# Mixture of experts in seven passes: the pass of the four smallest experts moves from fourth to sixth place

## The chip, the cores and the metric

The kernel runs on one core of a Trainium2 chip. The core has TensorE (matmuls), VectorE, ScalarE and GpSimd for elementwise work, SyncE, whose queue issues the large loads here, and 16 DMA engines. The metric is the device time of one execution in microseconds, as a median over runs.

## The reference

Two layers of a diffusion transformer over 256 latent tokens of 1024 features, with 256 context tokens beside them in the first layer. The first layer mixes tokens with latent attention and a gated linear recurrence, the second with a Hyena operator (long filters applied by Fourier transform between gates). Behind each mixer stands a mixture of 16 experts; each token takes two of them. Cut to what matters:

```
for layer in range(2):
    x = x + g1 * mixer[layer](modulate(rms_norm(x), sh1, sc1))
    h = modulate(rms_norm(x), sh2, sc2)
    gates = top2_in_best_group(sigmoid(h @ router_w))        # (256, 16)
    y = 0
    for e in range(16):
        act = silu(h @ w1[layer, e]) * (h @ w3[layer, e])    # 1024 -> 512
        y = y + gates[:, e:e+1] * (act @ w2[layer, e])       # 512 -> 1024
    x = x + g2 * y
return rms_norm(x, final_g)
```

Only the latent tokens' result is returned. All is float32. One expert has 6 MB of weights, one layer 96 MB, and no weight is used twice, so the two layers of experts fetch 192 MB from HBM.

## The kernel before

**Passes.** A layer of experts runs in seven passes, listed in `PASSES` (line 27). Six are pairs: two experts, with 64 token slots each, side by side in the 128 columns of TensorE. One is the quad: four experts with 32 slots each. Numbers 0 to 3 in the table are experts in a fixed order. Numbers 4 to 15 are places in an order sorted by token counts, which the kernel computes and loads into SyncE's registers (`chosen`); 4 to 7 are the four with fewest tokens. Both layers use the same table. In this text passes and places are counted from the first to the seventh; in the code `j` counts them from 0.

**One pass** (in `moe`) is: `up` with w1 (L1247, 64 matmuls for a quad, 32 for a pair), `silu`, `back` of the pass before (L1292, adds its result to x), fillers, `up` with w3, `times`, `turn` (transposes, L1262), fillers, `down` 0 and 1 with w2 (L1275) and `weigh`. In every second pass (`j` = 1, 3, 5) the tokens of the next two passes are fetched behind the w3 part: `place` builds a 0/1 matrix, `gather` multiplies it in (L1218), `slots` (L1234, L1236) makes the matrix and the gate values for the way back. So the gather for the fifth and sixth pass stands in the fourth place, and the gather for the seventh alone in the sixth.

**Fillers.** In the first layer `fill` runs pieces of the second layer's Hyena filters between these parts: an item is a filter step (L1439 two projections on TensorE, then eight VectorE instructions at L1448 to L1457 and one on GpSimd, then L1466 transposes and a copy on ScalarE) or a step of the Fourier butterflies (L1495, L1496). Its counts stand in `FJ`, one triple for each place, and belong to the place, whatever the pass. Places four and five have seven items each (in those with a gather one item is dropped from the second count), place six has five. In the second layer there are none.

**Weights.** `moe_tiles` lists a layer's weights as tiles of 1 MB, in the order of `PASSES`: for a pair 4 of w1, 4 of w3, 4 of w2; for the quad 8, 8 and 8; 98 loads for a layer, because four tiles of the last pass are cut in halves. In this text they are numbered from 0 in that order. `emit` (L219) issues them on SyncE, in order, from one queue; each waits there until the buffer that it goes to is free. In the first layer the buffers are a ring of ten in the steady state (nine of `w` and one of `x`), so that a tile can be issued when the tile ten places ahead has been used. In the second layer the ring has 18 (`sp`, `w` and `x`). An expert chosen by count has its address from a register; the tiles of the first two passes do not need it.

```
PASSES = ((0, 1), (2, 3), (8, 9), (4, 5, 6, 7), (10, 11), (12, 13), (14, 15))
FJ = ((0, 1, 1), (0, 1, 1), (1, 1, 2), (2, 3, 3), (1, 3, 3), (2, 1, 3), (2, 4, 1))
            fill(fills[j][0])
            up(j, "w3", first, firsts)
            times(j)
            if j % 2 and j < LAST:
                d = j // 2 + 1
                place(d, pos, firsts)
                gather(d, firsts)
```

The order of instructions on each engine is set by the order of the program and by a scheduler that moves single instructions a little; the order of weight tiles on SyncE follows `PASSES` alone.

Of the kernel before, what the change touches and what calls it, by code (L numbers as in the profile page):

```python
# [23 lines left out]
LOW = 32  # L24
STATIC = 4
DYN = 16 - STATIC
PASSES = ((0, 1), (2, 3), (8, 9), (4, 5, 6, 7), (10, 11), (12, 13), (14, 15))
LAST = len(PASSES) - 1
QUAD = 4
NW = 9  # L30
# [136 lines left out]
def build(tc, A, dbg=None, stop=None):  # L167
# [54 lines left out]
    def get(key):  # L222
        while key not in made:
            emit(1)
        used[0] = max(used[0], index[key] + 1)
        return made[key]
# [53 lines left out]
    def moe_tiles(l):  # L280
        for j, es_ in enumerate(PASSES):
            for nme in ("w1", "w3"):
                for kk in range(2):
                    for e in es_:
                        yield ((nme, l, e, kk), expert(nme, l, e, kk * 512, 4, 0, 512), (128, 4, 512))
            for h in range(2):
                for e in es_:
                    if j < LAST:
                        yield (("w2", l, e, h), expert("w2", l, e, h * 256, 2, 0, 1024), (128, 2, 1024))
                    elif h == 0:  # L290
                        yield (("w2", l, e, 0), expert("w2", l, e, 0, 4, 0, 512), (128, 4, 512))
            if j == LAST:
                for h in range(2):
                    for e in es_:
                        yield (("w2", l, e, 1 + h), expert("w2", l, e, h * 256, 2, 512, 512), (128, 2, 512))
# [875 lines left out]
    def moe(l, route, ws, filler=None, fills=((0, 0, 0),) * 8, budget=0, late=None, prepare=None, finish=None):  # L1171
# [22 lines left out]
        pairs = tuple(((2 * j, 2 * j + 1), CAP) for j in range(8))  # L1194
        firsts = tuple((es_, 128 // len(es_)) for es_ in PASSES)

# [114 lines left out]
        def first(nme, e, k, n=0):  # L1311
            if nme == "w2" and e in PASSES[LAST]:
                return get((nme, l, e, 1 + k // 2))[:, k % 2, :] if n else get((nme, l, e, 0))[:, k, :]
            nk = 2 if nme == "w2" else 4
            return get((nme, l, e, k // nk))[:, k % nk, n * 512:n * 512 + 512]
# [454 lines left out]
```

## Time and profile before

| | |
|---|---|
| time, median of 3 runs | 961.68 us (961.64, 965.34, 961.68) |
| the profiled execution's own time | 964.56 us |
| its span | 962.8 us |
| TensorE busy | 868.0 us, 90% |
| VectorE busy | 477.8 us, 50% |
| bytes moved | 289.33 MB, mean 301 GB/s |
| first layer of experts, on TensorE | 285.1 to 541.0 us |
| second layer of experts, on TensorE | 728.3 to 952 us |

The profile is of one execution; the span runs from its first to its last instruction. Busy time says how long an engine worked, not whether anyone waited for it; the waits and the stretches say that. The DMA share is the mean busy share of the 16 DMA engines, and rows that show a little more than 1 stand for full.

### The profile page before, as it was taken

The page shows a single profiled execution, that of the slowest core. Times are in us where ns is not written, and L with a number is a line of the kernel's source. Part 1 is how long each engine was busy: PE and PEld are TensorE (multiplying, and loading weights), DVE is VectorE, ACT ScalarE, POOL GpSimd, SP SyncE. Part 2 cuts the span into 40 slices and gives each one's busy share as a digit, 9 for nine tenths or more (in the row PEclk, how much of TensorE's full clock was granted, in tenths as well). Part 3 has the DMA queues.
Part 4 walks back from the last instruction along what each step waited for, and adds up shares of the span by engine and source line. Part 5 has one row for each costly group of instructions (what it writes and reads, how often), then busy time and mean ns, then how long its engine had stood idle before and what let it go on. Part 6 is the DMA issues. An engine that isn't in the chain of part 4 may idle for free. (4 is left out here: it accounts for less than half of the span.)

```text
span 962.8 us, 10887 instructions
## 1 busy us (share of the span) xinstructions
PE 868.0 (90%) x3992; PEld 458.1 (48%) x3992; DVE 477.8 (50%) x1119; ACT 231.9 (24%) x451; POOL 25.9 (3%) x29
## 2 busy tenths in 40 slices
PE   3898999999969999889999599999959999988984
PEld 1445755575543543433343288677545352422431
DVE  5349775763364445345622469976163241322123
ACT  3266414430231222122211312211031020100112
POOL 0000000000010000001100000000020000000000
PEclk9899999998969999999999799999978999999997
DMA  9946679469479889999999866842285999999994
GB/s 353 336 183 240 224 263 354 166 223 367 170 271 324 333 324 386 383 400 396 391 362 347 308 228 253 314 167 88 87 298 189 391 396 386 401 392 396 396 386 148
DMA packets 130568, 289.33 MB, mean 301 GB/s; under 512 B 6828, under 2 KB 8876, under 8 KB 130500
## 3 DMA queue, kind: packets, MB, share of 16 engines
q1 hardware_dynamic: 129428, 286.39, 81.5%
q10 hardware_dynamic: 1072, 2.10, 0.7%
q8 instruction: 35, 0.57, 0.2%
q14 instruction: 33, 0.27, 0.1%
HBM read 287.42 MB, written 1.05 MB: 300 GB/s over the span
## 5 line engine op out<-in xcount | busy, mean ns | idle before, releaser
L1247 PE MATMUL ps<-w,xe 128*64 128x512 f32 (+1 forms) x696 | 174.3, 597 | 2.8 <-DMA w<-in_moe_w 2.8
L1247 PEld LDWEIGHTS ps<-w,xe 128*64 128x64 f32 (+1 forms) x696 | 50.0, 129 | 88.0 <-issue 79.2
L1275 PE MATMUL ps<-w,at 128*64 128x512 f32 (+1 forms) x344 | 87.1, 597 | 4.5 <-DMA w<-in_moe_w 2.7
L1591 PE MATMUL ps<-xt,w 128*128 128x256 f32 x384 | 88.2, 388 | 1.8 <-ACT xt L1554 1.8
L1591 PEld LDWEIGHTS ps<-xt,w 128*128 128x128 f32 x384 | 74.2, 195 | 14.4 <-ACT xt L1554 2.1
L1294 DVE TENSOR_TENSOR x<-x,ps 128x512 f32<-128x512 f32 x56 | 37.0, 684 | 68.1 <-PE ps L1292 68.1
L442 DVE SCALAR_TENSOR_TENSOR e<-w,sg,e 128x512 f32<-128x512 f32 x91 | 67.0, 746 | 5.2 <-DMA w<-in_ada_w 4.1
L1281 DVE SCALAR_TENSOR_TENSOR ye<-ps,gs,grow 128x512 f32<-128x512 f32 x28 | 21.0, 748 | 83.9 <-PE ps L1275 83.9
L1247 PE MATMUL ps<-sp,xe 128*64 128x512 f32 (+1 forms) x216 | 55.5, 600 | 1.5 <-DMA sp<-in_moe_w 1.5
L1275 PEld LDWEIGHTS ps<-w,at 128*64 128x64 f32 (+1 forms) x344 | 26.9, 130 | 50.8 <-issue 40.3
L1283 ACT ACTIVATE yeh<-ye 128x512 fp32r<-128x512 f32 x28 | 17.6, 630 | 118.2 <-DVE ye L1281 118.2
L1257 DVE TENSOR_TENSOR th<-th,ps 128x512 f32<-128x512 f32 x14 | 9.6, 688 | 60.5 <-PE ps L1247 60.5
L1247 PE MATMUL ps<-x,xe 128*64 128x512 f32 (+1 forms) x112 | 37.5, 596 | 1.6 <-DMA x<-in_moe_w 1.6
L1218 PE MATMUL ps<-P,yh 128*128 128x256 f32 (+1 forms) x128 | 35.9, 313 | 2.8 <-DVE P L1203 2.8
L1218 PE MATMUL ps<-P,yl 128*128 128x256 f32 (+1 forms) x128 | 35.0, 307 | 0.0
L1223 ACT ACTIVATE xe<-ps,modc 128x256 f32<-128x256 f32 (+1 forms) x32 | 16.5, 540 | 70.0 <-DVE xe L1221 69.9
L1218 PEld LDWEIGHTS ps<-P,yh 128*128 128x128 f32 x128 | 27.9, 218 | 9.6 <-issue 7.1
L844 PE MATMUL ps<-hT,w 128*128 128x512 f32 x64 | 31.0, 643 | 1.2 <-DMA w<-in_ev_w_in 1.2
L1247 PEld LDWEIGHTS ps<-sp,xe 128*64 128x64 f32 (+1 forms) x216 | 16.0, 132 | 28.1 <-issue 24.4
L510 PE MATMUL ps<-w,x 128*128 128x512 f32 x64 | 28.4, 595 | 0.7 <-ACT x L1605 0.7
L510 PE MATMUL ps<-w,mix 128*128 128x512 f32 x64 | 28.8, 598 | 0.0
L1218 PEld LDWEIGHTS ps<-P,yl 128*128 128x128 f32 x128 | 27.8, 217 | 1.7 <-issue 1.7
(350 smaller groups left out, 1313.9 us busy)
## 6 DMA issues: line engine op xcount, KB each, us to landing
w<-in_moe_w SPq DMA_DIRECT2D x126, 1024.0 KB, 13.8
w<-in_ada_w SPq DMA_DIRECT2D x48, 1024.0 KB, 7.1
sp<-in_moe_w SPq DMA_DIRECT2D x41, 1024.0 KB, 14.2
x<-in_moe_w SPq DMA_DIRECT2D x21, 1024.0 KB, 14.5
w<-in_od_w_in SPq DMA_DIRECT2D x12, 1024.0 KB, 7.1
w<-in_ev_w_in SPq DMA_DIRECT2D x4, 1024.0 KB, 11.0
w<-in_ev_w_out SPq DMA_DIRECT2D x4, 1024.0 KB, 6.8
w<-in_moe_w SPq DMA_DIRECT2D x8, 512.0 KB, 9.8
```

The source lines that it names most:

```text
L442: V.scalar_tensor_tensor(eh, w[hf], c, eh, op0=OP.mult, op1=OP.add)
L510: T.matmul(po[t][n], a[:, k, t * 128:t * 128 + 128], b[:, n * 512:n * 512 + 512], start=(k == korder[0] and i == 0), stop=(k == korder[-1] ...
L844: T.matmul(uxp[b], get(("wux", hf))[:, k % 4, b * 128:b * 128 + 128], hT[hf][:, k % 4, :], start=(k == 0), stop=(k == KD - 1))
L1218: T.matmul(p[:, kk * w:kk * w + w], (yl if i % 2 else yh)[:, t, k * 128:k * 128 + 128], P[:, t, :w], start=(i == 0), stop=(i == 3))
L1223: S.activation(e[:, k, :w], p[:, w:2 * w], AF.Identity, scale=sc[:, k:k + 1], bias=sh[:, k:k + 1])
L1247: T.matmul(p[room * i:room * i + room, :], xe[j // 2][:, k, o:o + room], weight(nme, e, k), start=(k == 0), stop=(k == KD - 1), tile_posit ...
L1257: V.tensor_tensor(act[j], act[j], hid[j, "w3"], op=OP.mult)
L1275: T.matmul(p[room * i:room * i + room, :], act[j][:, o:o + room], weight("w2", e, k, n), start=(k == 0), stop=(k == 3), tile_position=(0, ...
L1281: V.scalar_tensor_tensor(e, po[j, n], gs[j], grow[l, 5][:, n * 512:n * 512 + 512], op0=OP.mult, op1=OP.mult)
L1283: S.activation(h, e, AF.Copy)
L1294: V.tensor_tensor(xs, xs, p, op=OP.add)
L1591: T.matmul(pb, w[:, k % 4, b * 128:b * 128 + 128], hT[:, k, :], start=(k == 0 and b % 2 == 0), stop=(k == KD - 1 and b % 2 == 1))
```

## The change

One line: the quad stands in the sixth place of the table, and the two pairs (10, 11) and (12, 13) move ahead of it. Each pass keeps its experts and its slots. What belongs to a place (the fillers, the gathers, the last pass's halves of w2) stays there.

```
-PASSES = ((0, 1), (2, 3), (8, 9), (4, 5, 6, 7), (10, 11), (12, 13), (14, 15))
+PASSES = ((0, 1), (2, 3), (8, 9), (10, 11), (12, 13), (4, 5, 6, 7), (14, 15))
```

TensorE, first layer, around the start of the fourth pass. Up to there its order is the same in both kernels. `w` is a weight tile, `xe` the gathered tokens, `at` the turned hidden values; 32x512 is a matmul for the 32 slots of one expert of the quad, 64x512 one for the 64 slots of an expert of a pair. Before:

```order
L1275 MATMUL ps_2369<-w_2355,at_2308 64x512
L1275 MATMUL ps_2369<-x_2358,at_2308 64x512
L1247 MATMUL ps_2384<-w_2385,xe_2047 32x512
L1247 MATMUL ps_2384<-w_2388,xe_2047 32x512
L1247 MATMUL ps_2384<-w_2391,xe_2047 32x512
L1292 MATMUL ps_2436<-yeh_2365,st_2093 128x512
L1292 MATMUL ps_2436<-yel_2367,st_2093 128x512
L1247 MATMUL ps_2384<-w_2394,xe_2047 32x512
```

With the change:

```order
L1275 MATMUL ps_2367<-w_2353,at_2306 64x512
L1275 MATMUL ps_2367<-x_2356,at_2306 64x512
L1247 MATMUL ps_2382<-w_2383,xe_2047 64x512
L1247 MATMUL ps_2382<-w_2386,xe_2047 64x512
L1247 MATMUL ps_2382<-w_2383,xe_2047 64x512
L1247 MATMUL ps_2382<-w_2386,xe_2047 64x512
L1247 MATMUL ps_2382<-w_2383,xe_2047 64x512
L1247 MATMUL ps_2382<-w_2386,xe_2047 64x512
```

Behind the same down matmuls stand a pair's matmuls, on two weight tiles in turn, where the quad's stood on four tiles in turn.

TensorE, first layer, behind the gather of the fourth pass: the slots (L1234, L1236), then fillers. `a2T` and `q` belong to the filter steps, `th` is the hidden part. Before:

```order
L1234 MATMUL ps_2585<-kc,P_2535 128x128 x2
L1236 MATMUL ps_2585<-rg_1524,P_2535 128x2 x2
L1234 MATMUL ps_2595<-kc,P_2535 128x128 x2
L1236 MATMUL ps_2595<-rg_1524,P_2535 128x2 x2
L1439 MATMUL ps_2605<-a2T,w_363_1927 128x256
L1247 MATMUL ps_2485<-w_2492,xe_2047 32x512
L1439 MATMUL ps_2606<-a2T,w_363_1927 128x256
L1466 MATMUL ps_2623<-kc,q_2474 128x128 x4
L1439 MATMUL ps_2629<-a2T,w_451_2311 128x256
L1247 MATMUL ps_2485<-w_2495,xe_2047 32x512
L1247 MATMUL ps_2485<-w_2486,xe_2047 32x512
L1247 MATMUL ps_2485<-w_2489,xe_2047 32x512
```

With the change:

```order
L1234 MATMUL ps_2545<-kc,P_2485 128x128 x2
L1236 MATMUL ps_2545<-rg_1524,P_2485 128x4 x2
L1439 MATMUL ps_2557<-a2T,w_363_1927 128x256
L1439 MATMUL ps_2558<-a2T,w_363_1927 128x256
L1466 MATMUL ps_2575<-kc,q_2448 128x128 x4
L1439 MATMUL ps_2581<-a2T,w_451_2309 128x256
L1439 MATMUL ps_2582<-a2T,w_451_2309 128x256
L1466 MATMUL ps_2599<-kc,q_2571 128x128 x4
L1262 MATMUL ps_2605<-kc,th_2407 128x128 x4
L1439 MATMUL ps_2616<-a2T,w_451_2309 128x256
L1439 MATMUL ps_2617<-a2T,w_451_2309 128x256
L1466 MATMUL ps_2634<-kc,q_2595 128x128 x4
```

Before, the fillers stood between the w3 matmuls of the quad. Now these are done ahead of the gather's end, and the filter steps stand one behind the other, with only the turn (L1262) between them.

SyncE, first layer, in the tiles of the fourth pass (128x4x512 is a tile of w1 or w3, 128x2x1024 one of w2; the rows of the ISA are waits). Before:

```order
L219 DMA w_2418<-in_moe_w 128x4x512
L219 ISA
L219 DMA w_2486<-in_moe_w 128x4x512
L219 ISA
L219 DMA w_2489<-in_moe_w 128x4x512
L219 ISA
L219 DMA w_2492<-in_moe_w 128x4x512
L219 ISA
L219 DMA w_2495<-in_moe_w 128x4x512
L219 ISA
L219 DMA w_2510<-in_moe_w 128x4x512
L219 ISA
```

With the change:

```order
L219 DMA w_2475<-in_moe_w 128x4x512
L219 ISA
L219 DMA w_2657<-in_moe_w 128x2x1024
L219 ISA
L219 DMA w_2660<-in_moe_w 128x2x1024
L219 ISA
L219 DMA w_2665<-in_moe_w 128x2x1024
L219 ISA
L219 DMA w_2668<-in_moe_w 128x2x1024
L219 ISA
L219 DMA w_2695<-in_moe_w 128x4x512
L219 ISA
```

At the same place in the queue the pair's four w2 tiles are reached after eight tiles of w1 and w3, where the quad had sixteen. The quad's 24 tiles come 24 tiles later. The number of tiles and of buffers is the same.

## Rows read from the trace of the kernel before

**Rows 1.** The page: busy tenths in 40 slices of the span.
```profile
PE   3898999999969999889999599999959999988984
...
DMA  9946679469479889999999866842285999999994
```

**Rows 2.** First layer's passes: length, PE, PEld, DVE, ACT, POOL busy (instructions), clock, DMA share, GB/s.
```profile
285.10:303.90 18.80, 18.62 (x92) 6.66 (x93) 7.25 (x23) 1.31 (x4) 0.97 (x1) 1.00 0.71 243
303.90:335.10 31.20, 31.20 (x164) 15.42 (x162) 13.76 (x34) 7.40 (x15) 0.74 (x1) 1.00 0.96 359
335.10:370.10 35.00, 34.15 (x156) 13.67 (x152) 16.97 (x39) 6.94 (x13) 2.42 (x3) 1.00 0.89 324
370.10:428.90 58.80, 53.50 (x295) 21.18 (x293) 23.80 (x59) 13.44 (x27) 3.48 (x4) 1.00 1.04 390
428.90:467.20 38.30, 37.19 (x157) 14.87 (x157) 23.51 (x55) 10.21 (x20) 4.47 (x5) 1.00 1.04 393
467.20:507.20 40.00, 37.96 (x173) 16.95 (x172) 15.06 (x32) 6.89 (x14) 1.69 (x2) 1.00 0.99 370
507.20:541.00 33.80, 31.32 (x134) 11.88 (x130) 12.74 (x22) 8.22 (x18) 0.00 (x0) 1.00 0.99 363
```

**Rows 3.** TensorE's waits, 370.1 to 428.9: who waited for whom, total, times, longest.
```profile
PE ps L1247 <- DMA w<-in_moe_w: 1.9, 1, 1.9
PE ps L1275 <- DMA w<-in_moe_w: 1.3, 2, 0.7
```

**Rows 4.** SyncE's queue, waits from 370 to 545, columns as in rows 3.
```profile
SPq L219 <- PE ps L1247: 44.8, 18, 7.1
SPq L219 <- PE ps L1275: 36.8, 9, 9.2
```

**Rows 5.** Second layer's second, third and sixth passes, columns as in rows 2.
```profile
752.40:782.40 30.00, 29.47 (x153) 14.36 (x152) 10.99 (x25) 5.04 (x10) 0.00 (x0) 1.00 1.04 394
782.40:806.50 24.10, 22.85 (x102) 8.51 (x99) 6.99 (x11) 2.24 (x4) 0.00 (x0) 1.00 1.04 386
...
884.20:916.90 32.70, 30.19 (x147) 13.51 (x145) 8.56 (x17) 3.54 (x9) 0.00 (x0) 1.00 1.04 394
```

**Rows 6.** The same stretch for gather L1218, then slots L1236, alone.
```profile
370.10:428.90 58.80, 4.36 (x32) 3.94 (x32) 1.00 1.04 390
...
370.10:428.90 58.80, 1.01 (x8) 1.05 (x8) 1.00 1.04 390
```

**Rows 7.** Groups on VectorE, 285 to 541: filter steps (busy, mean ns, idle before).
```profile
L1448 DVE TENSOR_TENSOR e<-e,ps 128x256 f32<-128x256 f32 x32 | 12.9, 416 | 5.2 <-PE ps L1439 3.5 <-ACT e L1442 0.9 <-issue 0.7
L1450 DVE TENSOR_REDUCE l<-e 128x1 f32<-128x512 f32 x16 | 10.9, 679 | 0.1
...
L1456 DVE TENSOR_TENSOR q<-e 128x256 f32<-128x256 f32 x16 | 8.0, 500 | 1.4 <-PE ps L1466 1.2
L1453 DVE TENSOR_SCALAR e<-e,l 128x512 f32<-128x512 f32 x16 | 7.7, 484 | 0.4
```

**Rows 8.** TensorE's timeline at the first layer's end: start, duration, instruction, idle before.
```profile
517.78 7.09 PE L1247 MATMUL ps<-w,xe 128*64 128x512 f32 x32
...
540.14 0.88 PE L1528 MATMUL ps<-kc,x 128*128 128x128 f32 x6 [0.16 <-DVE x L1294]
548.49 1.19 PE L1542 MATMUL ps<-v,ones 128*128 128x128 f32 x4 [7.47 <-DVE v L1541]
551.52 8.82 PE L1591 MATMUL ps<-xt,w 128*128 128x256 f32 x27 [1.83 <-ACT xt L1554]
```

**Rows 9.** The tile issued at 335.3 us, with no other in flight.
```profile
DMA to landing us min/median/max: 5.0/5.0/5.0
```

**Rows 10.** TensorE's timeline, a stretch of the quad, then of the fifth pass.
```profile
396.13 3.62 PE L1247 MATMUL ps<-w,xe 128*32 128x512 f32 x26
...
433.30 3.65 PE L1247 MATMUL ps<-w,xe 128*64 128x512 f32 x14
```

**Rows 11.** The tile issued at 507.4 us: tile 91, the last of w3.
```profile
DMA to landing us min/median/max: 5.6/5.6/5.6
```

## The prediction

> **What bounds the kernel now.** The page comes first. Its two lines of slices show that in most of the span TensorE is busy for nine tenths or more and the DMA engines are as full [rows 1]. So neither alone is the bound, and the two layers have to be read pass by pass.
>
> The table by stretches, one row for each expert pass of the first layer, shows who is ahead in each [rows 2]. From the second pass on the DMA share is 0.89 to 1.04, and TensorE is busy for all but 0 to 5 us of each pass. The fourth pass, the quad, is the long one: 58.8 us. It must fetch 24 tiles of 1 MB where a pair fetches 12. In the fifth pass, where nothing holds it up, the stream moves 393 GB/s, so that a tile of 1,048,576 bytes takes 2.67 us. 24 tiles are 64 us, 12 tiles 32 us. A pair here takes 35 to 40 us of TensorE, because the fillers of the Hyena filters lie in it, so TensorE is slower than the stream in a pair and faster in the quad. What lets the two even out is the ring of ten tiles.
>
> The waits confirm this: TensorE waits for weights in the quad, but for only 1.9 and 1.3 us [rows 3], whereas SyncE, which issues the weights, waits 44.8 and 36.8 us for matmuls of L1247 and L1275 to give slots back [rows 4]. Ring and stream are thus just about in balance: the stream runs ahead of a pair, loses its lead in the quad, and gets it back behind it.
>
> The second layer has no fillers. Its rows (three of the four pairs between the first and the last) have a share of 1.04 at 386 to 394 GB/s, with 22.85 to 30.19 us of TensorE's busy time [rows 5]: less than the stream's 32 us. There the stream is the bound, and it has 18 slots to run ahead.
>
> **The change, part by part.** No matmul is added or removed, and no byte. Three things move.
>
> 1. *Second layer.* The same 98 tiles go through the same queue, and every pair, with a gather or without, needs at most 30.2 us of TensorE [rows 5], less than 32 us of stream. No order of the passes makes a slot late, and the end of the last pass is set by the stream. Cost: 0; bounds: 0 to 0.3 us.
>
> 2. *First layer, fourth and fifth passes.* They are pairs now. The filler and gather stay with the place in the program, not with the experts: the fourth place has seven filler items and the gather of two passes, the fifth seven items. What a pair with seven items takes is the old fifth pass: 38.3 us [rows 2], nearly all of it busy. The gather and the slots that the fourth place has as well cost 4.36 and 1.01 us [rows 6]; with about 1 us for their transposes and hand-overs the new fourth pass takes 38.3 + 4.4 + 1.0 + 1.0 = 44.7 us, against 58.8. The fifth takes 38.3 us. The quad thus starts at E = 370.1 + 44.7 + 38.3 = 453.1 us. Unknown is what VectorE does to it: a filter step costs VectorE 2 x 416 + 679 + 484 + 500 ns [rows 7], 2.5 us beside short instructions, and the steps now stand one behind the other where the long quad's matmuls lay between them. From the old fifth pass, where VectorE is busy for 23.5 of 38.3 us, I bound it at 0 to 4 us and take 0.8. E becomes 453.9 (450.5 if the hand-overs hide and the items fit better; 457 at worst).
>
> 3. *The quad in the sixth place.* Both pairs take longer than their 32 us of stream, so at E the ring is full and the stream stands still. Of the ten slots four hold the fifth pass's w2 tiles; only six hold tiles of the quad (its numbers 60 to 65 of the layer, counted from 0). The seventh, tile 66, waits for the first w2 slot, which comes free when three quarters of the down matmuls are done. That stage takes 7.1 us (the w3 up of the last pass shows the same 32 matmuls in 7.09 [rows 8]), so the slot is free at E - 1.8. An issue that finds no other transfer in flight lands 5.0 us later [rows 9]: tile 66 lands at E + 3.2. From there the stream is the bound: TensorE needs for the quad no more than for a pair (26 matmuls of a quad take 3.62 us and 14 of a pair 3.65, since four run side by side instead of two [rows 10]), about 40 us with its gather and items as in the old sixth pass [rows 2], against 64 us of stream.
>
> The end follows from tile 91, the last w3 tile of the last pass. It is 25 tiles later: E + 3.2 + 25 x 2.67 = E + 70.0. The second half of that pass's w3 up needs it. Before, this half began 521.3 us into the span (halfway through the 7.09 us from 517.78 [rows 8]), and TensorE's work of the layer ended 19.7 us later, at 541.0. So the layer ends at E + 89.7 us.
>
> With E = 453.9 this is 543.6, with 453.1 it is 542.8; with 450.5, 540.2; with 457, 546.7. Before it was 541.0. **Sum: +2.6 us in the first layer (-0.8 to +5.7), 0 in the second.** What follows the layer is a wait for VectorE of 7.47 us [rows 8], which begins from the same last tokens, so it moves along. The Hyena's input weights are issued behind the experts' and come some 8 us later, but the projection starts only at 551.5 and spends 8.82 us on its first 27 matmuls [rows 8], so its tiles are used slowly: hidden, and estimated at 1 us at most if not.
>
> **A rule weighed.** The rows say that the before kernel alternates: a stretch in which TensorE is ahead (the quad, 58.8 us for 64 us of stream) stands between stretches in which the stream is ahead (35 to 40 us for 32) [rows 2]. The new order puts two of the latter in a row and the quad behind both. The Trainium skill, Perfetto Trace Analysis, section Optimization Strategy, says that a kernel whose most contended engine changes over time may gain if such stretches are interleaved; by that rule the new order, which interleaves less, loses. The trace gives it the sign but a small size: before, tile 91 was issued at 507.4 and landed 5.6 us later [rows 11], 8.3 us ahead of its use at 521.3, and most of what the stream loses comes out of that.
>
> **Against the time.** The profiled execution took 964.56 us, 1.8 us beside its span of 962.8, and is 2.9 us above the median of the runs shown, 961.68. I add 2.6 to the median: 964.3 us.
>
> **Rivals.**
> *A, clearly slower.* The VectorE chain of the items, no longer spread over 58.8 us, makes TensorE wait in the fourth and fifth passes, and the projection waits for its weights too. For it: the 2.5 us of VectorE that each filter step needs in a row. Against it: the old fifth pass had seven items in 38.3 us too, and TensorE was busy for 37.19 us of them [rows 2]. E = 457 and the whole 1 us behind it give 546.7 + 1.0, 6.7 us more: 968.4 us.
> *B, faster.* The ring has enough of the quad at E. Each tile more than six that has landed then is worth 2.67 us; from three more on (nine) the end is 543.6 - 8.0 = 535.6, 5.4 us less: 956.3 us. That decides it, and it needs more slots than the ten less the four that the fifth pass still holds. Only TensorE would bound it then: 44.7 + 38.3 + 40.0 + 33.8 from 370.1, 526.9 us, 14 us less. Against it: the waits of SyncE for slots are all over these passes [rows 4].
> *C, nothing.* The stream is the bound throughout and only its total counts: 961.7 us. For it: shares of 1.0 and more in both layers. Against it: in the first layer it would need the stream not to stop in front of the quad.
>
> **How the numbers follow.** My forecast, loss of a few us, 0.57; A 0.28; B 0.05; C 0.10. Range: from the lower bound of the sum, 961.68 - 0.8 = 960.9, to A's 968.4; it leaves out B and the upper tail of A. 0.5% is 4.8 us, about what a measurement of this kernel can tell from no change. So faster 0.05 (B); same: C, and nearly all of my forecast (up to 966.5), 0.63; slower: A and the upper end of the forecast, 0.32.
>
> **What would show it.** In the new profile the fourth pass should take 43 to 47 us and the fifth 37 to 40. The stream should show a gap of some 10 us ahead of the quad, its share well under 1.0 in the fourth and fifth passes, and TensorE should wait for weights in the quad and in the last pass, some 16 us in all (the 89.7 us from E to the end less 40 and 33.8 of work), where it waited 3. The layer's last matmul should lie at 541 to 546. The second layer should look the same, within 1 us. I am wrong if the fourth pass takes over 48 us (A), if the quad shows few waits for weights (B), or if the second layer's share falls below 1 in its middle.

## The result, and the profile after

| | before | with the change |
|---|---|---|
| time, median of 8 runs each | 961.66 us (960.33 to 965.34) | 968.82 us (967.89 to 971.55) |
| ratio | | 1.0066, 95% interval 1.0050 to 1.0081 |
| span of the profiled execution | 962.8 us | 969.7 us |
| first layer of experts ends on TensorE | 541.0 us | 549.5 us |
| from the start of the fourth pass to there | 170.9 us | 177.6 us |

The kernel is 6 to 7 us slower. The profiled execution of before took 964.56 us, that with the change 971.55, which is the slowest of its eight. The two differ by 1.8 us already at the start of the fourth pass (370.1 and 371.9), where nothing is changed yet. Times below are therefore counted from the start of the fourth pass where they are compared.

The slices of the page first (answer to [rows 1], with the line of GB/s under it). The digits 77 in the 18th and 19th slice of the DMA line, 293 and 270 GB/s, stand where before there was 99:

```profile
DMA  9946689469479889977999978762265999999994
GB/s 354 338 174 238 223 279 357 171 209 373 144 272 326 331 327 393 333 293 270 389 405 387 385 262 299 253 224 88 87 251 205 392 396 396 392 391 387 405 387 151
```

The four passes from the fourth on (columns as in [rows 2]): two pairs, the quad, the last pair.

```profile
371.90:418.60 46.70, 43.29 (x200) 20.30 (x198) 24.70 (x61) 13.54 (x27) 2.92 (x4) 0.96 0.84 310
418.60:457.70 39.10, 36.62 (x161) 14.79 (x157) 22.71 (x55) 10.81 (x21) 4.09 (x5) 0.96 0.86 324
457.70:511.60 53.90, 47.29 (x269) 17.83 (x267) 14.34 (x31) 6.90 (x14) 1.89 (x2) 1.00 1.03 392
511.60:549.50 37.90, 32.67 (x133) 11.80 (x132) 12.71 (x21) 7.65 (x18) 0.00 (x0) 1.00 1.05 387
```

The pairs take 46.7 and 39.1 us, with a DMA share of 0.84 and 0.86 where it was 1.04, and with a granted clock of 0.96, where every pass of before had 1.00. The quad takes 53.9 us, the last pass 37.9 against 33.8.

Where the share went is seen in three short stretches: behind tile 53, and in front of tile 66 of the quad.

```profile
411.10:417.00 5.90, 5.90 (x28) 1.92 (x28) 2.53 (x5) 2.13 (x4) 0.00 (x0) 1.00 0.00 0
417.00:422.40 5.40, 5.40 (x28) 1.73 (x24) 1.24 (x2) 0.63 (x1) 0.00 (x0) 1.00 0.77 266
452.50:461.50 9.00, 9.00 (x60) 2.69 (x58) 3.78 (x8) 1.95 (x4) 0.00 (x0) 1.00 0.47 156
```

For 5.9 us not a byte moves, and then it takes another 5.4 us until tile 54 has landed; from the landing of tile 65 at 452.5 to that of tile 66 at 461.5 it is 9.0 us. Less the 2.67 us that one tile takes anyway, the stream loses 8.6 + 6.3 = 14.9 us, where the prediction expected one gap of some 10 us ahead of the quad. TensorE is busy all that time. Tile 66 itself, issued at 456.1, 1.6 us ahead of the quad's start at 457.7 (answer to [rows 9]):

```profile
L219 SPq DMA_DIRECT2D w<-in_moe_w x1: 373/373/373, 456.1 to 456.1; - x1
...
DMA to landing us min/median/max: 5.4/5.4/5.4
```

TensorE's waits from 370 to 550 us (answer to [rows 3], where no wait for VectorE in L1466 appeared; of the 1.9 us at L1495, 0.7 lie in the pairs):

```profile
PE ps L1247 <- DMA w<-in_moe_w: 5.8, 4, 1.7
PE ps L1466 <- DVE l L1451: 2.7, 2, 1.4
PE ps L1466 <- DVE q L1457: 2.4, 2, 1.8
PE ps L1495 <- ACT spec L1469: 1.9, 2, 1.2
...
PE ps L1275 <- DMA w<-in_moe_w: 1.3, 2, 0.7
```

And SyncE's (answer to [rows 4]): the longest wait for a down part to give a slot back is now 19.9 us, where it was 9.2.

```profile
SPq L219 <- PE ps L1247: 48.3, 21, 7.6
SPq L219 <- PE ps L1275: 48.0, 9, 19.9
```

TensorE behind the gather of the fourth pass: three filter steps in a row, then butterflies (columns as in [rows 8]).

```profile
399.81 0.70 PE L1439 MATMUL ps<-a2T,w 64*128 64x256 f32 x4
401.88 0.72 PE L1466 MATMUL ps<-kc,q 128*128 128x128 f32 x4 [1.38 <-DVE l L1451]
...
402.97 0.70 PE L1439 MATMUL ps<-a2T,w 64*128 64x256 f32 x4
405.02 0.74 PE L1466 MATMUL ps<-kc,q 128*128 128x128 f32 x4 [1.35 <-DVE l L1451]
406.45 2.07 PE L1495 MATMUL ps<-spec,fixed 128*128 128x512 f32 x2 [0.69 <-ACT spec L1469]
408.31 1.69 PE L1496 MATMUL ps<-spec,fixed 128*128 128x512 f32 x2
409.84 1.02 PE L1495 MATMUL ps<-spec,fixed 128*128 128x512 f32 x2
```

Two waits for VectorE of 1.38 and 1.35 us, one of 0.69 for ScalarE, and then the same pair of matmuls takes 2.07 and 1.69 us, two rows further on 1.02: TensorE has fallen to the lower of its two clocks, 1.2 GHz, behind the waits and come back to 2.4. In the stretches of 4 us from 404 and from 408 us the granted clock is 0.78 and 0.79. The fifth pass has the same picture, with waits of 0.59 and 1.77 us, a clock of 0.60 from 444 to 448, and 2.07 and 1.53 us.

The fall in the fourth pass is not in every execution. The run e1_first, described below, has the same program in this layer and nearly the same waits there, but the matmuls behind them take 1.12 us, and the pass takes 45.1 us at a granted clock of 1.00:

```profile
401.85 0.74 PE L1466 MATMUL ps<-kc,q 128*128 128x128 f32 x4 [1.35 <-DVE l L1451]
403.28 1.12 PE L1495 MATMUL ps<-spec,fixed 128*128 128x512 f32 x2 [0.69 <-ACT spec L1469]
...
368.70:413.80 45.10, 41.69 (x198) 19.64 (x196) 24.67 (x61) 13.54 (x27) 2.92 (x4) 1.00 0.86 319
```

In e3_fifth and e12_ring9, whose fourth pass is also that of the change, it takes 45.2 us at 1.00. In the fifth pass the clock falls in e1_first and e12_ring9 too (0.96 in both).

The end of the layer (answer to [rows 8]): the second half of the last w3 part waits for tile 91, which landed at 529.7.

```profile
529.70 3.65 PE L1247 MATMUL ps<-w,xe 128*64 128x512 f32 x14 [1.63 <-DMA w<-in_moe_w]
...
548.58 0.88 PE L1528 MATMUL ps<-kc,x 128*128 128x128 f32 x6 [0.16 <-DVE x L1294]
556.98 1.19 PE L1542 MATMUL ps<-v,ones 128*128 128x128 f32 x4 [7.52 <-DVE v L1541]
```

The second layer is as it was: its last weight tile lands 323.9 us after its first (628.7 and 952.6), before 324.3 (621.0 and 945.3), and its two new pairs in the fourth and fifth place have full DMA:

```profile
815.00:845.60 30.60, 30.07 (x156) 14.64 (x153) 10.59 (x23) 5.04 (x10) 0.00 (x0) 1.00 1.04 393
845.60:873.10 27.50, 26.25 (x118) 9.64 (x116) 7.93 (x13) 2.87 (x5) 0.00 (x0) 1.00 1.04 393
```

In this execution the first layer ends 8.5 us later than before and the span is 6.9 us longer. Of the difference 0.7 us came back in the Hyena projection, which starts 8.5 us later (560.0 and 551.5) and ends 7.7 us later (672.4 and 664.6). Its group on the page is 86.9 us of busy time, 88.2 before:

```profile
L1591 PE MATMUL ps<-xt,w 128*128 128x256 f32 x384 | 86.9, 385 | 1.8 <-ACT xt L1554 1.8
```

### The profile page after: what moved, and what is told of

The parts are those of the page before. It is cut to its first block, busy times and chain, and to the rows that moved or that the text cites. A ratio compares the mean times of both kernels' runs of the same rounds, so it can differ in the third digit from the quotient of the medians.

```text
span 969.7 us, 10892 instructions
## 1 busy us (share of the span) xinstructions
PE 868.4 (90%) x3992; PEld 459.1 (47%) x3992; DVE 476.9 (49%) x1119; ACT 232.1 (24%) x451; POOL 25.2 (3%) x29
## 3 DMA queue, kind: packets, MB, share of 16 engines
HBM read 287.42 MB, written 1.05 MB: 297 GB/s over the span
## 5 line engine op out<-in xcount | busy, mean ns | idle before, releaser
L1247 PE MATMUL ps<-w,xe 128*64 128x512 f32 (+1 forms) x632 | 155.4, 596 | 5.8 <-DMA w<-in_moe_w 5.8
L1275 PE MATMUL ps<-w,at 128*64 128x512 f32 (+1 forms) x408 | 99.2, 597 | 5.5 <-DMA w<-in_moe_w 3.2
L1591 PE MATMUL ps<-xt,w 128*128 128x256 f32 x384 | 86.9, 385 | 1.8 <-ACT xt L1554 1.8
L1247 PEld LDWEIGHTS ps<-w,xe 128*64 128x64 f32 (+1 forms) x632 | 45.5, 129 | 87.3 <-issue 74.1
L1247 PE MATMUL ps<-sp,xe 128*64 128x512 f32 (+1 forms) x264 | 70.5, 641 | 6.4 <-DMA sp<-in_moe_w 6.4
L1275 PEld LDWEIGHTS ps<-w,at 128*64 128x64 f32 (+1 forms) x408 | 28.9, 128 | 62.8 <-issue 49.0
L1247 PE MATMUL ps<-x,xe 128*64 128x512 f32 (+1 forms) x128 | 44.5, 595 | 0.0
L1247 PEld LDWEIGHTS ps<-sp,xe 128*64 128x64 f32 (+1 forms) x264 | 20.0, 137 | 43.4 <-issue 31.5
L1218 PE MATMUL ps<-P,yh 128*128 128x256 f32 (+1 forms) x128 | 35.9, 314 | 2.8 <-DVE P L1203 2.8
L1218 PE MATMUL ps<-P,yl 128*128 128x256 f32 (+1 forms) x128 | 34.8, 306 | 0.0
L1218 PEld LDWEIGHTS ps<-P,yh 128*128 128x128 f32 x128 | 28.0, 218 | 9.6 <-issue 5.5
L1218 PEld LDWEIGHTS ps<-P,yl 128*128 128x128 f32 x128 | 28.0, 219 | 0.8 <-issue 0.8
```

What stands on the lines that cost most here:

```text
L1218: T.matmul(p[:, kk * w:kk * w + w], (yl if i % 2 else yh)[:, t, k * 128:k * 128 + 128], P[:, t, :w], start=(i == 0), stop=(i == 3))
L1247: T.matmul(p[room * i:room * i + room, :], xe[j // 2][:, k, o:o + room], weight(nme, e, k), start=(k == 0), stop=(k == KD - 1), tile_posit ...
L1275: T.matmul(p[room * i:room * i + room, :], act[j][:, o:o + room], weight("w2", e, k, n), start=(k == 0), stop=(k == 3), tile_position=(0, ...
L1591: T.matmul(pb, w[:, k % 4, b * 128:b * 128 + 128], hT[:, k, :], start=(k == 0 and b % 2 == 0), stop=(k == KD - 1 and b % 2 == 1))
```

## The experiments

Each kernel was timed in five rounds against the kernel before on the same chip; ratios are to that, with their 95% interval. Medians of before differ by up to 2.5 us between chips, so ratios are compared, not microseconds. "Layer time" is the time from the start of the fourth pass to the end of the first layer's experts, 170.9 us before and 177.6 with the change.

| run | order, fillers in places 4, 5, 6 | ratio | layer time, us |
|---|---|---|---|
| the change | quad sixth; 7, 7, 5 | 1.0066 (1.0050 to 1.0081) | 177.6 |
| e1_first | the same, second layer old | 1.0045 (1.0025 to 1.0065) | 176.1 |
| e2_second | first layer old | 0.9994 (0.9977 to 1.0011) | 171.9 |
| e4_spread | quad sixth; 7, 7, 5, spread | 1.0008 (0.9990 to 1.0026) | 172.5 |
| e5_fills | quad sixth; 4, 4, 10 | 0.9932 (0.9906 to 0.9959) | 165.4 |
| e6_before_fills | quad fourth; 10, 4, 5 | 0.9956 (0.9937 to 0.9975) | 166.6 |
| e3_fifth | quad fifth; 7, 7, 5 | 1.0016 (0.9994 to 1.0038) | 171.9 |
| e7_after_nofill | quad sixth; none | 1.0626 (1.0594 to 1.0658) | |
| e8_before_nofill | quad fourth; none | 1.0620 (1.0586 to 1.0655) | |
| e12_ring9 | quad sixth; 7, 7, 5; ring of nine | 1.0086 (1.0070 to 1.0102) | 178.4 |
| e14_before_ring9 | quad fourth; 7, 7, 5; ring of nine | 1.0014 (1.0004 to 1.0024) | 170.5 |
| e13_more | quad sixth; 3, 3, 13 | 0.9949 (0.9928 to 0.9969) | |
| e15_both | quad sixth; 4, 4, 10, spread | 0.9909 (0.9890 to 0.9929) | 164.1 |

### Which layer loses: one layer in each order

The table of passes becomes one for each layer, and is indexed by the layer where it is read.

```
-PASSES = ((0, 1), (2, 3), (8, 9), (10, 11), (12, 13), (4, 5, 6, 7), (14, 15))
+PASSES = (((0, 1), (2, 3), (8, 9), (10, 11), (12, 13), (4, 5, 6, 7), (14, 15)),
+          ((0, 1), (2, 3), (8, 9), (4, 5, 6, 7), (10, 11), (12, 13), (14, 15)))
...
-        for j, es_ in enumerate(PASSES):
+        for j, es_ in enumerate(PASSES[l]):
```

Expected of the first layer alone:

> The new order in the first layer of experts only, the old one in the second. Theory (the stream stands still in front of the quad, in the first layer alone, and the second layer is bound by the stream whatever the order): the whole loss, 967.5 to 970 us, as the changed kernel. Rival (part of the loss is made in the second layer, by its own two pairs ahead of the quad): at least 2 us less, 964 to 966.5 us.

Expected of the second layer alone (the two tables exchanged):

> The new order in the second layer only, the old one in the first. Theory: 961 to 963 us, as before, with the last weight tile landing within 1 us of the kernel before (945.3 us into its span). Rival (second layer takes part): 964 us or more.

Measured: 1.0045 and 0.9994. The first layer alone has a loss whose interval overlaps that of the whole change, and its layer time is 176.1 us; the second alone is the kernel before, with its last tile 325.1 us after its first (946.3 and 621.2). So the second layer takes no part that these runs can tell; the upper end of the interval of e2_second leaves it 1 us.

### VectorE and the start of the quad: the same fillers, spread

Two more places for fillers, in the middle of the w3 part and between the two down parts; the counts of the fourth and fifth pass stay at seven.

```
-FJ = (..., (2, 3, 3), (1, 3, 3), (2, 1, 3), (2, 4, 1))
+FJ = (..., (1, 2, 1), (1, 1, 1), (2, 1, 3), (2, 4, 1))
+MORE = ((0, 0), (0, 0), (0, 0), (2, 2), (2, 2), (0, 0), (0, 0))
...
-            up(j, "w3", first, firsts)
+            up(j, "w3", first, firsts, range(4)), fill(more[j][0]), up(j, "w3", first, firsts, range(4, KD))
...
-                down(j, 1, first, firsts)
+                fill(more[j][1]), down(j, 1, first, firsts)
```

> The changed order, with the same seven fillers in the fourth and in the fifth pass, but spread: two more places, in the middle of the w3 matmuls and between the two down parts, so that no three filter steps stand in a row. Theory that the time beyond my sum came from VectorE (5.1 us of waits of TensorE for VectorE in the filter steps, and matmuls at half clock behind them, some 3 us): the two passes get 4 to 8 us shorter, and since everything behind hangs on the start of the quad, the kernel too: 961 to 965 us. Rival (the start of the quad does not matter, only the number of tiles behind it): no change, 967.5 to 970 us.

Measured: 1.0008, nearly all of the loss gone. The passes from the fourth on:

```profile
370.30:413.70 43.40, 42.46 (x198) 19.57 (x196) 24.11 (x61) 13.54 (x27) 3.30 (x4) 1.00 0.91 335
413.70:451.10 37.40, 36.03 (x161) 13.84 (x157) 22.79 (x55) 10.66 (x21) 4.27 (x5) 1.00 0.90 337
451.10:505.00 53.90, 47.19 (x269) 17.25 (x268) 14.87 (x31) 6.90 (x14) 1.67 (x2) 1.00 1.03 393
505.00:542.80 37.80, 32.61 (x132) 11.75 (x132) 12.61 (x21) 7.62 (x18) 0.00 (x0) 1.00 1.05 387
```

and TensorE's waits in the two pairs:

```profile
PE ps L1466 <- DVE q L1457: 2.1, 2, 1.1
PE ps L1495 <- ACT spec L1469: 0.2, 1, 0.2
```

The pairs are 43.4 and 37.4 us, 3.3 and 1.7 less than with the change, the clock is 1.00 again, and the waits for VectorE and ScalarE are 2.3 us instead of 5.8. Some of that is the clock of the one execution with the change: against e1_first, with 45.1 and 39.4 us, the pairs are 1.7 and 2.0 us shorter. The quad starts at 451.1, and the layer ends 91.7 us behind that; with the change it was 549.5 - 457.7 = 91.8, in e1_first 544.8 - 453.2 = 91.6. The end follows the start of the quad one to one, as the theory has it, and not the rival.

### What the order needs: fillers moved into the quad

```
-FJ = (..., (2, 3, 3), (1, 3, 3), (2, 1, 3), (2, 4, 1))
+FJ = (..., (1, 2, 2), (1, 2, 1), (3, 4, 4), (3, 4, 1))
```

> The changed order, with six fillers moved from the fourth and fifth pass into the quad's (4, 4 and 10 items instead of 7, 7 and 5) and one more in the last. Theory (a pair with fillers is slower than its 32 us of stream, the quad faster than its 64): pairs near 37 and 32 us, the quad starts 10 us earlier, and the end follows it: 956 to 960 us, faster than before. Rival (a race lost by the order as such, whatever fills the pairs; or a bound by the sum of TensorE's work): 966 to 970 us.

Measured: 0.9932, faster than before.

```profile
369.90:409.40 39.50, 37.12 (x184) 17.35 (x182) 19.32 (x49) 10.85 (x22) 2.37 (x3) 1.00 0.99 367
409.40:442.30 32.90, 32.12 (x134) 11.80 (x130) 14.31 (x31) 6.44 (x12) 1.47 (x2) 1.00 1.03 385
442.30:498.70 56.40, 51.66 (x304) 21.32 (x302) 27.39 (x65) 12.88 (x26) 4.97 (x6) 0.94 1.01 379
498.70:535.30 36.60, 33.28 (x140) 13.13 (x136) 14.05 (x24) 8.79 (x19) 0.00 (x0) 1.00 1.05 387
```

Both pairs are near their 32 us of stream (39.5 and 32.9; the fourth has the gather), the share is 0.99 and 1.03, and five more fillers in the quad cost it 2.5 us against the change. The quad starts 72.4 us after the fourth pass, with the change 85.8.

A like move with the old order, so that the quad in the fourth place has ten items too, three of them from the fifth pass:

```
-FJ = (..., (2, 3, 3), (1, 3, 3), (2, 1, 3), (2, 4, 1))
+FJ = (..., (3, 4, 4), (1, 2, 1), (2, 1, 3), (2, 4, 1))
```

> The old order (quad fourth), with three fillers moved from the fifth pass into the quad's (10 and 4 items instead of 7 and 7). Theory (with the quad fourth the stream never stops, and TensorE's work sets the end, wherever the fillers are): within 2 us of before, 960 to 965 us by the pace of the chip. Rival (moving fillers into the quad's pass is worth the same whatever the order, so the gain of the run with the moved fillers has nothing to do with the quad's place): 4 us or more below before.

Measured: 0.9956. Here my expectation was wrong, and the time is the rival's.

```profile
368.70:428.10 59.40, 54.51 (x319) 22.99 (x317) 32.55 (x82) 17.20 (x36) 6.46 (x7) 0.94 0.99 369
428.10:462.30 34.20, 32.53 (x135) 12.55 (x134) 15.22 (x31) 6.45 (x12) 1.46 (x2) 1.00 1.04 394
```

Three more fillers lengthen the quad from 58.8 to 59.4 us and shorten the pass behind it from 38.3 to 34.2. TensorE's idle time in the quad hardly changes, 5.3 us before (53.5 busy of 58.8) and 4.9 now, but what it waits for does: 3.2 us for weights and 1.3 for ScalarE before; now 4.1 us for VectorE in the filter steps and none for weights. The 64 down matmuls of L1275 for the quad fill 8.8 us where they filled 11.5. So the added steps fill time that the quad spent on weights that came late, and the old order had not used that room either. A gain from fillers that lie in the quad is thus there wherever it stands, but it is not the same in both orders: in layer time 170.9 - 166.6 = 4.3 us with three items moved, 177.6 - 165.4 = 12.2 with six, because the new order also had to win back what its pairs had lost. That the quad does better sixth than fourth, once the fillers fit, is not shown: the intervals of 0.9932 and 0.9956 overlap.

### One pair more ahead of the quad instead of two

```
-PASSES = ((0, 1), (2, 3), (8, 9), (10, 11), (12, 13), (4, 5, 6, 7), (14, 15))
+PASSES = ((0, 1), (2, 3), (8, 9), (10, 11), (4, 5, 6, 7), (12, 13), (14, 15))
```

> The quad in the fifth place, behind one sorted pair more than before, in both layers; fillers as they were. Theory: one standstill of the stream instead of two. The quad starts some 47 us behind the fourth pass's start, its 18 tiles that are not in the ring land 3.8 + 17 x 2.73 us after, and 3.6 us of down, 40.0 and 33.8 us for the last two passes follow: layer end some 3.5 us later than before, 963.5 to 967 us. Rival (the loss comes with the second pair, or only where the gather meets the quad's wait): within 1 us of before.

Measured: 1.0016, an interval that holds no change and a loss of 3.7 us both; the time alone does not decide. The passes:

```profile
371.00:416.20 45.20, 41.83 (x202) 19.51 (x199) 24.92 (x61) 13.54 (x27) 3.13 (x4) 1.00 0.87 322
416.20:469.80 53.60, 47.18 (x254) 15.38 (x252) 22.21 (x55) 10.85 (x21) 4.48 (x5) 0.94 1.03 392
469.80:509.10 39.30, 37.02 (x172) 16.72 (x173) 15.03 (x31) 6.27 (x13) 1.70 (x2) 1.00 1.04 392
509.10:542.90 33.80, 31.32 (x134) 11.83 (x130) 12.84 (x22) 8.21 (x18) 0.00 (x0) 1.00 1.05 387
```

The pair ahead of the quad has a share of 0.87, one standstill. The quad takes 53.6 us, where the terms for it in the sum make 3.8 + 17 x 2.73 + 3.6 = 53.8, and the last two passes 39.3 and 33.8, where they took 40.0 and 33.8 before. The layer time is 1.0 us above before, where I had expected 3.5: the pair with the gather took 45.2 us instead of some 47, and the quad and the sixth pass 0.2 and 0.7 us less than worked out. Tile 91 landed at 519.8, 3.5 us ahead of its use at 523.3, where before it was 8.3 us ahead. One standstill is thus nearly paid for by the slack, two are not.

### No fillers at all

`FILLS = 0` in both orders; the filter steps then run behind the first layer.

> The changed order with no fillers at all in the passes; the filter steps run behind the first layer, which makes the kernel some 50 to 60 us longer. Its partner is the same with the old order. Theory (without fillers every pair needs less than 32 us of TensorE, the stream is the bound as in the second layer and the order does not matter): both within 2 us of each other. Rival (the order costs by itself, by the gathers and the chosen addresses): the changed order 5 to 8 us longer.

> The partner of the run above: the old order without fillers in the passes. Theory: within 2 us of the changed order without fillers. Rival: 5 to 8 us shorter than that.

Measured: 1.0626 and 1.0620. The change without fillers, from 365 to 520 us:

```profile
365.00:520.00 155.00, 133.75 (x606) 47.87 (x604) 32.84 (x63) 14.82 (x29) 0.00 (x0) 0.96 1.04 392
```

and the old order without fillers:

```profile
365.00:520.00 155.00, 133.88 (x607) 48.77 (x606) 33.05 (x61) 14.87 (x31) 0.00 (x0) 0.96 1.04 392
```

The stream is full in both, and the order costs nothing that these runs can tell (each interval is some 3 us to either side). What the order costs is thus what the fillers do in the pairs.

### The depth of the ring

`NX = (0, 3)` instead of `(1, 3)` takes the one `x` slot away, in the first layer alone.

> The changed order with one slot fewer in the first layer's ring (nine instead of ten). Theory (at the start of the quad the ring holds all slots less the fifth pass's four; each slot is one tile of 2.67 us): at the quad's start tile 64 is the last one in, tile 65 lands first behind the standstill, and the layer's end is some 2.7 us further behind the quad's start: 94 to 95 us instead of 91.8; the kernel 2 to 3 us above the changed one, ratio to before 1.008 to 1.010. Rival (the ring's depth does not matter, only fillers and VectorE do): as the changed kernel, 1.0066.

> The partner: the old order with a ring of nine. Theory: the stream does not stand still ahead of the quad's last tiles, and tile 91 had 8.3 us of slack, so the lost slot is paid out of the slack: within 1.5 us of before. Rival (a slot is worth the same in any order): 2 to 3 us above before.

Measured: 1.0086 with the new order and 1.0014 with the old. Quad and last pass of the new order with nine slots:

```profile
455.20:511.10 55.90, 47.63 (x268) 17.86 (x266) 14.30 (x31) 6.90 (x14) 1.88 (x2) 0.97 1.03 394
511.10:549.00 37.90, 32.73 (x133) 11.83 (x132) 12.72 (x21) 7.61 (x18) 0.00 (x0) 1.00 1.05 387
```

The layer ends 93.8 us behind the quad's start at 455.2, 2.0 us more than with ten slots, a little under the expected 94 to 95. The trace shows this; the ratios alone do not, since the intervals of 1.0086 and of the change's 1.0066 overlap. The layer time is only 0.8 us above the change's, because the quad starts 84.6 us behind the fourth pass, where the clock did not fall here. Now tile 65 is the first behind the standstill: issued at 453.5, landed 5.0 us later. The old order's layer time is 170.5 us, no longer than before: its stream did not stand still there (a share of 1.04 from 370 to 500 us), and the lost slot is paid out of the slack of tile 91, which landed at 514.9, 6.6 us ahead of its use instead of 8.3.

### More fillers into the quad, and both edits together

3, 3 and 3 items in the third to fifth pass, 13 in the quad:

```
+FJ = (..., (1, 1, 1), (1, 2, 1), (1, 1, 1), (4, 5, 5), (3, 4, 1))
```

> The changed order with the fillers moved further: 3, 3 and 3 items in the third to fifth pass, 13 in the quad (7, 7, 5 in the changed kernel; 4, 4, 10 in the earlier run). Theory: the pairs are then at or below their 32 us of stream, it hardly stops, and what is left is the stream itself; 0 to 2 us below the earlier run, ratio to before 0.990 to 0.994. Rival (thirteen items with VectorE's 2.5 to 3 us each no longer fit beside the quad's matmuls): the quad's pass gets longer than its stream, above 64 us, ratio 0.996 or more.

Measured: 0.9949, between the two. The fifth and sixth passes:

```profile
402.80:433.90 31.10, 30.23 (x135) 11.68 (x132) 15.23 (x35) 5.27 (x11) 2.43 (x3) 1.00 1.04 386
433.90:498.60 64.70, 58.49 (x319) 24.11 (x318) 32.44 (x77) 16.85 (x34) 5.87 (x7) 0.92 0.98 370
```

The pair is at 31.1 us, below its stream, but the quad is at 64.7 us with a share of 0.98, and from 370 to 540 us TensorE does not wait for weights at all. So it is no longer the stream that sets it, and further fillers in the quad have no wait for weights left to fill.

Moved and spread (4, 4 and 10 items, over five places in each pass):

```
+FJ = (..., (1, 1, 1), (1, 0, 1), (2, 2, 3), (3, 4, 1))
+MORE = ((0, 0), (0, 0), (0, 0), (1, 1), (1, 1), (2, 2), (0, 0))
```

> The changed order with both edits that helped: 4, 4 and 10 fillers in the fourth to sixth pass as in the run with moved fillers, and spread over the two more places (middle of the w3 matmuls, between the down parts) in all three. Theory: TensorE's waits for VectorE in the filter steps, 5.6 us from 370 to 550 us in the run with moved fillers, mostly go; the layer ends up to 3 us earlier than there: ratio to before 0.990 to 0.993. Rival (the quad's end is set by the stream's 64 us, so that a wait less only moves the wait to the weights): as the run with moved fillers, 0.993 to 0.996.

Measured: 0.9909 (954.79 against 963.63 us), the fastest of all, and better than both kernels of this study by more than their intervals.

```profile
368.50:406.20 37.70, 37.70 (x182) 17.19 (x180) 19.93 (x49) 11.06 (x22) 2.38 (x3) 1.00 1.03 381
406.20:439.80 33.60, 32.82 (x136) 11.86 (x134) 14.00 (x30) 5.88 (x12) 1.73 (x2) 1.00 1.03 384
439.80:494.70 54.90, 50.72 (x304) 20.76 (x303) 26.70 (x65) 13.83 (x28) 4.99 (x6) 0.97 1.01 382
494.70:532.60 37.90, 34.05 (x137) 12.63 (x136) 14.17 (x23) 8.52 (x20) 0.00 (x0) 1.00 1.05 387
```

The share is 1.01 to 1.05 in all four passes. Against the moved fillers alone the layer time is 1.3 us less, less than the 3 expected; the intervals of the two runs overlap, so the part of the spreading on top is not shown. The old order with ten fillers in the quad and the same spreading was not run, so whether the quad's place has a part in this gain stays open.

## Why the prediction was right or wrong

The direction and the mechanism were right; the size was not. The forecast was +2.6 us, and "within 0.5%" had the largest chance. Measured is a ratio of 1.0066, slower by more than 0.5%, with an interval that begins at 1.0050. The median of 968.82 lies 0.4 us above the range, 1.0066 times the 961.68 of the forecast, 968.0, just inside it. The upper end of that range is A's price and not the sum's.

**Second layer: 0.** Right, by the profile and by e1_first and e2_second.

**Fourth and fifth passes.** Forecast 44.7 and 38.3 us and 0.8 for VectorE, measured 46.7 and 39.1: the quad's start is 2.0 us later than forecast. The term "I bound it at 0 to 4 us and take 0.8" was mis-sized within its bounds: TensorE waited 5.8 us for the filter steps' VectorE and ScalarE in the two passes. The sum also had no term for the lower clock that can follow such waits: (2.07 - 1.02) + (1.69 - 1.02) = 1.7 us in the fourth pass, 1.05 + 0.51 = 1.6 in the fifth. e4_spread has 2.3 us of these waits and no low clock, and its two passes are 5.0 us shorter. The fall of the clock in the fourth pass is not in every execution, though: e1_first, with the same first layer, does not have it, and its quad starts 453.2 - 368.7 = 84.5 us behind the fourth pass, 0.7 later than forecast (84.6 in e12_ring9). This is the place of rival A. Its price was nearly the measured time, which is in part luck, since only part of its mechanism happened: the quad started 85.8 us behind the fourth pass (A: 86.9), and the projection did not wait for its weights.

**First landing.** Forecast E + 3.2, measured E + 3.8: the slot came free 1.6 us ahead of the quad's start instead of 1.8, and the transfer took 5.4 us, not 5.0. 0.6 us.

**Tile 91.** Forecast 25 x 2.67 = 66.8 us behind tile 66, measured 529.7 - 461.5 = 68.2, or 2.73 us for each. (Of the last pass two tiles are cut, into four halves; both lie behind tile 91.) The step of 2.67 came from a pass with 393 GB/s; the quad had 392 and the last pass 387, which makes 2.67 to 2.71 us. 1.4 us in sum, and where the rest of it went no row here shows.

**From tile 91 to the end.** Forecast 19.7 us, measured 549.5 - 529.7 = 19.8.

Together 2.0 + 0.6 + 1.4 + 0.1 = 4.1 us above the forecast of 2.6: the 6.7 us that the layer lost in this execution, half of the miss at the start of the quad and half behind it. In e1_first the layer lost 5.2 us (176.1 against 170.9), with 0.7 of the miss at the start of the quad and 91.6 - 89.7 = 1.9 behind it. So what was sized too small in both is the step from the quad's start to the layer's end, the first landing and the 25 tiles up to tile 91, by some 2 us; the start of the quad adds 0.7 us to that, or 2.0 where the clock falls in the fourth pass. All terms erred to the same side.

**The ring of six tiles at the quad's start.** Right: tile 66 is the first to land behind the standstill, with nine slots it is tile 65, and the end follows the quad's start with ten slots at a fixed 91.6 to 91.8 us. Rival B, which needed nine tiles, did not happen. Rival C did not either.

**Waits for weights, some 16 us.** Wrong as put: the list of waits names 3.3 + 1.3 in the quad and 2.5 in the last pass, 7.1 us. Against the old sixth and seventh pass the two are 91.8 - 73.8 = 18.0 us longer, but only 7.3 us of that are idle time (11.8 against 4.5); 10.7 us are busy time. There the prediction's step from the 26 matmuls in 3.62 us [rows 10] to 40 us for the whole quad fails. A single matmul of the quad still takes 597 ns, but while the tiles land one by one fewer of them run side by side: behind the landing of a tile at 484.5 us two of them take 1.04 us, behind the next, at 487.2, 26 take 3.62.

**The rule.** The rule of the Trainium skill (Perfetto Trace Analysis, Optimization Strategy), that interleaving stretches with different bounds may help, agrees with the runs: the order that interleaves less lost 0.66%, with two standstills, and e3_fifth, with one pair more ahead of the quad and one standstill, lost little or nothing. But e5_fills, with the same order, shows what to interleave: with more of the fillers in the quad and fewer in the pairs, each pass is nearer to its own stream, and the order of the passes no longer costs anything that was shown.

## What to carry to other kernels

Where a stream of weights runs through a ring, as here, the order of passes mattered as far as passes were slower than the stream for longer than the ring could hold: compare each pass's compute time with its own bytes (here 46.7 us beside 32 us of stream for the first pair, 53.9 beside 64 for the quad), and count the tiles that the ring can hold when the long fetch begins. Optional work is best tried in the pass that waits for its weights, spread so that no chain of a second engine stands in a row: the run with both was 0.9% faster than before, where the order alone had lost 0.7%. When a sum is made of durations from undisturbed rows, look at which of them will meet a wait. And before a term is explained from one profile, look at the same pass in other runs that share it: 1.3 of the 2.0 us missed at the quad's start were in one execution alone.

## What the runs showed of the hardware

TensorE's clock can fall behind a few short waits, and need not. With the change, behind waits of 1.38, 1.35 and 0.69 us with filter steps and a turn between them, two matmuls took 2.07 us for 1.02 and the next two 1.69, so that 3.4 us of waits cost 1.7 us more. In e1_first, e3_fifth and e12_ring9 the waits there were the same to 0.05 us, and the same matmuls took 1.12 or 1.13 and 1.02 us, at a granted clock of 1.00. Behind the waits of 0.59 and 1.77 us in the fifth pass the clock fell in all three traces that have it: 2.07 and 1.53 us with the change, 1.85 and 1.91 in e1_first, 1.71 and 1.91 in e12_ring9. The Trainium skill (TensorE: Matmul & The Clock Gate, Part 1) says that the clock follows how busy TensorE has been; where it fell in these passes, TensorE had waited just before.

A tile of 1 MB that meets an empty stream took 5.0 to 5.4 us from its issue to its landing, where in a full one a tile landed every 2.67 to 2.73 us on average: each standstill costs the idle time and this start besides.
